# A decoder block on one core: the PLE projection is moved between the halves of the output projection, with three smaller reorderings

## The chip, the cores and the metric

The kernel is one program on one core of a Trainium2 chip. The metric is the device time of one execution in microseconds (us). Before the change it is 344.85 us, the median of three runs (344.47 to 345.8). The profile shown here is of one further execution of the same kernel.

The core's engines run their own instruction streams in order and wait for each other through semaphores: TensorE (PE in the profile; PEld is its loading of weights), VectorE (DVE), ScalarE (ACT), GpSimd (POOL) and SyncE (SP), which here only issues DMA transfers.

## The reference

One transformer layer over 256 positions of width 1024, in float32:

```python
hn  = rmsnorm(h, g_attn)
qkv = hn @ w_in                                  # 1024 -> 3072, split into two groups of 8 heads
ya  = rmsnorm(merge_heads(dilated_mixture(qa, ka, va, slopes_a)), g_out_a)
yb  = rmsnorm(merge_heads(moba_attention(qb, kb, vb, slopes_b)), g_out_b)
h   = h + concatenate([ya, yb]) @ w_out
h   = h + square(relu(rmsnorm(h, g_mlp) @ w_up)) @ w_down      # 1024 -> 4096 -> 1024
gate = sigmoid(rmsnorm(h, g_ple) @ w_ple_gate + b_ple_gate)
h   = h + gate * (p @ w_ple_proj)                # p is 256 x 256: the per-layer embedding (PLE)
out = rmsnorm(h, g_final)
```

With 256 positions both attention groups are plain causal attention over 256 keys with a bias per head: for group A the ALiBi distance less the logarithm of how many of the three dilated branches hold the key, for group B the distance alone. The sum of squares behind each RMSNorm can be taken apart from the product it scales, which the kernel does throughout.

## The kernel before

**Split operands.** Every float32 matrix that enters a matmul is split into a high part (`hi`, a copy rounded to fp32r on ACT, L79 or L81) and a low part (`lo`, the rest, a subtraction on DVE, L86 or L88). A product is three matmuls (`mm3`, L209 to L211): hi by hi, hi by lo, lo by hi. Weights come in slabs of 1 MB through four raw buffers; a slab's load (L61, issued by SP) waits until the slab four places earlier has been split.

**Units.** The program is a list of units in the order in which PE works: the first (v of group A and q, k of pairs 0 and 1), q and k of pairs 2 and 3, v of group B, q and k of pairs 4 to 7 in two units, the output projection's half over group A (`o_steps(0)`), its half over group B (`o_steps(1)`), eight pairs of MLP units (up, down) with the PLE projection (`ple_steps`, 24 matmuls) after the first up unit, and two gate units. While a unit runs, the next unit's slabs are split.

**Attention.** A pair is two heads. For each of the eight pairs n: DVE scales q and k out of PSUM (L362), ACT and DVE split them (L366, L370), PE makes the scores (L400), DVE adds the bias and takes the minimum (L408, L411), ACT exponentiates (L418), DVE takes the reciprocal of the sums (L422), ACT and POOL scale the probabilities `pb` (L431, L429), PE transposes them (L451), ACT and DVE copy them out (L455), PE multiplies by v (L467, L468), ACT and DVE split the result y (L476, L485), and its squares are summed into `ysum` by POOL (L482). POOL also makes the bias tile of the next pair (L388, for group A also L390), in two buffers. At the end of each group `y_stats` sums `ysum` over partitions with PE (L330) and takes the power -0.5 on POOL (L241).

**What sets the order.** In the first six units the order on PE, DVE, ACT and POOL is written out: a planner keeps a clock that advances by a unit's cost per step, and each attention step is an event with a due time on that clock (`at`, `within`), issued in the program when the clock passes it. An engine then runs its instructions in that order, however late its inputs are. SP is not under this planner. After the sixth unit a scheduler orders the engines by itself.

**Start.** The first unit takes eight blocks k of x and weights as they arrive. `x_squares` sums the squares of x block by block (ACT L323, two buffers; DVE L324), and `x_stats` sums them over partitions on PE (L330) after step 30, that is between blocks 4 and 5.

**End.** `gate_out` (L793 to L820) closes each piece of the output: z, sigmoid, times `ple`, plus h, sum of squares, times the gain (POOL L809), and on a token tile's last piece the mean of squares (L813), its power -0.5 (POOL L814), the scaling (DVE L816, ACT L818, POOL L819) and two stores (L817, L820). Token tile 1 is last, in a piece of 256 columns.

Of the kernel before, what the change touches and what calls it, by code (L numbers as in the profile page):

```python
# [17 lines left out]
P = 128  # L18
S = 256
# [13 lines left out]
def block_kernel(ctx: ExitStack, tc: tile.TileContext, a: dict):  # L33
# [106 lines left out]
    def run_units(units):  # L140
        with tc.manual_schedule(engines=ORDERED):
            first_loads()
            first_splits()
            for i, u in enumerate(units[:6]):
                for s in units[i + 2].slabs:
                    s.load()
                for f in u.inserts.get(0, []):
                    f()
                if i:
                    t, d = clock[0], u.n * u.cost  # L150
                    pieces = [(s, p) for s in units[i + 1].slabs for p in range(s.n)]
                    for n, (s, p) in enumerate(pieces):
                        hi, lo = s.halves(p)
                        dt = d * (n / len(pieces) if i > 1 else 0.35 + 0.65 * n / len(pieces))
                        at(t + dt, hi)
                        at(t + dt + 1.1, lo)
                for j, step in enumerate(u.steps()):
                    if i:
                        clock[0] += u.cost
                        run_events(1e9)  # L160
                    for f in u.inserts.get(j + 1, []):
                        f()
            while any(e[2] for e in events):
                clock[0] = min(e[0] for e in events if e[2])
                run_events(1e9)
        for i, u in list(enumerate(units))[6:]:
# [25 lines left out]
    def first_splits():  # L192
        for k in range(KT):
            if k in (0, 1, 2, 4):
                x_split(k, k + (1 if k < 2 else 2))
            sv, sq = (slabs_in[u][k // 4] for u in range(2))
            for part in (slice(0, 0.5), slice(0.5, 1)) if k == 0 else [slice(0, 1)]:
                for f in sv.halves(k % 4, part):
                    f()
            for f in sq.halves(k % 4):  # L200
                f()
            if k == 4:
                x_split(6, 8)
            if k:
                x_squares({1: range(2), 2: range(2, 4), 4: range(4, 6), 5: range(6, 8)}.get(k, ()))
# [151 lines left out]
    def evac_qk(g, j, ps):  # L357
# [21 lines left out]
        at(max(t + dt + 2.4, 3.4 + 8.1 * n), lambda: scores(g, j), 0.75)  # L379
# [12 lines left out]
    def scores(g, j):  # L392
# [47 lines left out]
        if n < 7:  # L440
            within(5.2, lambda: make_bias((n + 1) // NPAIR, (n + 1) % NPAIR))
        within(7.4 if n < 7 else 6.2, lambda: turn(g, j), 0.7)
# [17 lines left out]
    def values(g, j):  # L460
# [29 lines left out]
        if j == NPAIR - 1:  # L490
            within(3.4, lambda: y_stats(g), 0.3)
# [85 lines left out]
    def late_pieces():  # L577
        for n in (2, 3):
# [6 lines left out]
             {30: [x_stats], 34: [x_diag] + early(0), 38: [x_bcast, lambda: make_bias(0, 0)], 41: early(1),  # L585
# [9 lines left out]
    hsum = st(4)  # L595

# [44 lines left out]
    class Lazy:  # L641
# [6 lines left out]
        Unit(slabs_out[:2], o_steps(0), None, 16, 0.681),  # L648
        Unit(slabs_out[2:], o_steps(1), {0: [alloc_aT2]}, 16),
# [6 lines left out]
    slab_ple = Slab(a["w_ple"], 2)  # L656
# [4 lines left out]
    def open_mlp():  # L661
# [6 lines left out]
        pT = m.tile([P, 2, S], F32, name="pTin")
        nc.sync.dma_start(pT, a["pT"])
        mp["p2"] = [m.tile([P, 2, S], F32R, name=f"p2{i}") for i in range(2)]  # L670
        nc.scalar.activation(mp["p2"][0], pT, AF.Copy)
        nc.vector.tensor_tensor(mp["p2"][1], pT, mp["p2"][0].bitcast(F32), op=ALU.subtract)
# [80 lines left out]
    def ple_steps():  # L753
        for t in range(2):
            for n in range(2):
                ps = bank()
                tok, col = slice(t * P, (t + 1) * P), slice(n * 512, (n + 1) * 512)
                for k in range(2):
                    mm3(ps, (mp["p2"][0][:, k, tok], mp["p2"][1][:, k, tok]),
                        (slab_ple.hi[:, k, col], slab_ple.lo[:, k, col]), k == 0, k == 1)  # L760
                    yield
                nc.scalar.copy(mp["ple"][:, t, col], ps)
# [23 lines left out]
    def gate_out(ps, t, i):  # L786
# [15 lines left out]
        nc.vector.tensor_tensor(sg, sg, mp["ple"][:, t, col], op=ALU.mult)  # L802
        nc.vector.tensor_tensor(h, h, sg, op=ALU.add)
        if last and t == 1:
            nc.vector.tensor_tensor_reduce(z, h, h, 1.0, 0.0, op0=ALU.mult, op1=ALU.add,
                                           accum_out=so[:, i : i + 1])
        else:
            nc.scalar.activation(z, h, AF.Square, accum_out=so[:, i : i + 1])
        nc.gpsimd.tensor_tensor(hg[:, col], h, gain[:, col], op=ALU.mult)  # L809
        if not last:  # L810
            nc.gpsimd.tensor_scalar(mean, so[:, i : i + 1], 1.0 / DM, mean if i else EPS, op0=ALU.mult, op1=ALU.add)
            return
        nc.vector.scalar_tensor_tensor(mean, so[:, i : i + 1], 1.0 / DM, mean, op0=ALU.mult, op1=ALU.add)  # L813
        nc.gpsimd.tensor_tensor(r, mean, mhalf[:, :1], op=ALU.pow)  # L814
        out = a["out"]
# [81 lines left out]
```

## Time and profile before

| what | value |
|---|---|
| median of three runs | 344.85 us |
| the profiled execution | 344.78 us, of which 343.0 us is the span from first to last instruction |
| busy PE, DVE, ACT, POOL | 329.6, 231.3, 205.0, 44.3 us |
| granted TensorE clock | mean 0.992 of full speed |
| chain that ended last | PE 76%, ACT 7%, DVE 6%, DMA 4%, POOL 3% |

A slice of the span in which PE shows 9 has no room to become shorter unless PE has less to do, and PE shows 9 nearly throughout. What an order can change is the time in which PE stands still: the waits, which the profile lists by line and by who ended them, and the tail after the last matmul. "Releaser" is the engine whose instruction ended a wait.

### The profile page before, as it was taken

Reading aid. Unit: us, or ns where it says so; the run is one execution under the profiler, and the core shown is the slowest. Engines: PE = TensorE matmul, PEld = TensorE weight load, DVE = VectorE, ACT = ScalarE, POOL = GpSimd, SP = SyncE. Lnnn points to the kernel's source line nnn. Section 1 sums busy time; section 2 is a strip of 40 time slices with the busy share of each in tenths; the row PEclk is TensorE's granted clock in tenths of the full one; section 3 lists DMA queues with packets and bytes.
Section 4 is the critical chain, followed back from the end, with each engine's and each line's share of the span. In section 5 each row is a group of like instructions: output and inputs, shape, how many; then the busy total and the mean of one; then the engine's idle time right before and its main releaser. Section 6 shows DMA issues by size and latency. Waiting matters only on the chain.

```text
span 343.0 us, 5168 instructions
## 1 busy us (share of the span) xinstructions
PE 329.6 (96%) x1932; PEld 282.3 (82%) x1932; DVE 231.3 (67%) x429; ACT 205.0 (60%) x402; POOL 44.3 (13%) x69
## 2 busy tenths in 40 slices
PE   8989999999998999999999999999999999999990
PEld 7879976899886788888888888888888888888890
DVE  3887966486666869768567585585755955658563
ACT  5775777757666767838354474463743836458431
POOL 0013147342122200000000000000000000000443
PEclk9999999999999999999999999999999999999996
DMA  7998864242436449553727528356193472700011
GB/s 201 367 350 332 302 224 138 107 137 112 149 106 204 144 166 333 185 218 125 259 109 257 232 53 316 124 196 263 38 345 139 139 248 105 246 0 1 2 61 61
DMA packets 10969, 60.84 MB, mean 177 GB/s; under 512 B 1216, under 2 KB 1984, under 8 KB 4416
## 3 DMA queue, kind: packets, MB, share of 16 engines
q1 hardware_dynamic: 10944, 60.51, 49.9%
q8 instruction: 15, 0.25, 0.3%
q14 instruction: 10, 0.08, 0.1%
HBM read 59.46 MB, written 1.05 MB: 176 GB/s over the span
## 4 chain that ended last, share of the span: by engine, by line
PE 76%; ACT 7%; DVE 6%; DMA 4%; POOL 3%; issue 2%; SPq 1%; POOLq 0%; DVEq 0%; ACTq 0%
PE ps L697 17%; PE ps L209 15%; PE ps L211 15%; PE ps L210 15%; PE ps L698 9%; DMA raw<-in_w_in 4%; DVE lo L86 2%; ACT pb L418 2%; ACT hi L79 2%; POOL pb L429 1%; PE ps L400 1%; PE ps L451 1%; PE ps L618 1%; DVE qklo L370 1%; POOL bias L390 1%
## 5 line engine op out<-in xcount | busy, mean ns | idle before, releaser
L86 DVE TENSOR_TENSOR lo<-raw,hi 128x1024 fp32r<-128x1024 f32 (+2 forms) x75 | 81.0, 1101 | 37.3 <-ACT hi L79 37.2
L697 PE MATMUL ps<-h,hi 128*128 128x512 f32 x256 | 90.9, 399 | 0.0
L79 ACT ACTIVATE hi<-raw 128x1024 fp32r<-128x1024 f32 (+2 forms) x75 | 69.3, 949 | 33.6 <-PE ps L211 27.2
L698 PE MATMUL ps<-h,lo 128*128 128x256 f32 x256 | 71.9, 281 | 0.0
L88 DVE SCALAR_TENSOR_TENSOR lo<-raw,head,hi 128x512 fp32r<-128x512 f32 x80 | 56.8, 748 | 10.1 <-ACT hi L81 10.1
L81 ACT ACTIVATE hi<-raw,head 128x512 fp32r<-128x512 f32 x80 | 53.0, 714 | 12.7 <-PE ps L211 6.9
L697 PEld LDWEIGHTS ps<-h,hi 128*128 128x128 f32 x256 | 48.1, 188 | 11.8
L209 PE MATMUL ps<-hi,u 128*128 128x512 f32 x128 | 50.3, 393 | 0.0
L211 PE MATMUL ps<-hi,u 128*128 128x512 f32 x128 | 50.0, 390 | 0.0
L210 PE MATMUL ps<-lo,u 128*128 128x512 f32 x128 | 49.9, 390 | 0.0
L698 PEld LDWEIGHTS ps<-h,lo 128*128 128x128 f32 x256 | 48.4, 189 | 0.3
L209 PE MATMUL ps<-x,hi 128*128 128x256 f32 x128 | 37.4, 292 | 0.4 <-ACT hi L79 0.4
L211 PE MATMUL ps<-x,lo 128*128 128x256 f32 x128 | 36.2, 283 | 0.2 <-DVE lo L86 0.2
L210 PE MATMUL ps<-x,hi 128*128 128x256 f32 x128 | 36.1, 282 | 0.0
L241 POOL TENSOR_TENSOR stat<-stat,mhalf 128x2 f32<-128x2 f32 x5 | 4.4, 875 | 227.4 <-DVE stat L240 227.4
L211 PEld LDWEIGHTS ps<-hi,u 128*128 128x128 f32 x128 | 24.0, 188 | 5.2
L209 PEld LDWEIGHTS ps<-hi,u 128*128 128x128 f32 x128 | 24.0, 188 | 5.0
L210 PEld LDWEIGHTS ps<-lo,u 128*128 128x128 f32 x128 | 24.1, 188 | 4.7
L209 PEld LDWEIGHTS ps<-x,hi 128*128 128x128 f32 x128 | 24.4, 191 | 1.8 <-ACT hi L79 0.7
L211 PEld LDWEIGHTS ps<-x,lo 128*128 128x128 f32 x128 | 24.4, 191 | 0.4 <-DVE lo L86 0.4
L210 PEld LDWEIGHTS ps<-x,hi 128*128 128x128 f32 x128 | 24.4, 191 | 0.2
L678 ACT COPY r<-ps 128x256 f32<-128x256 f32 x32 | 11.8, 367 | 19.7 <-PE ps L698 19.6
(130 smaller groups left out, 514.0 us busy)
## 6 DMA issues: line engine op xcount, KB each, us to landing
raw<-in_w_up SPq DMA_DIRECT2D x16, 1024.0 KB, 5.1
raw<-in_w_down SPq DMA_DIRECT2D x16, 1024.0 KB, 4.8
raw<-in_w_in SPq DMA_DIRECT2D x8, 1024.0 KB, 5.5
raw<-in_w_out SPq DMA_DIRECT2D x4, 1024.0 KB, 4.7
raw<-in_w_gate SPq DMA_DIRECT2D x4, 1024.0 KB, 5.3
raw<-in_w_in SPq DMA_DIRECT2D x4, 512.0 KB, 9.2
raw<-in_w_in SPq DMA_DIRECT2D x7, 256.0 KB, 6.5
h_sb<-in_x SPq DMA_DIRECT2D x1, 1024.0 KB, 6.9
```

What stands on the lines that cost most here:

```text
L79: nc.scalar.activation(h, r, AF.Copy)
L81: nc.scalar.activation(h, r, AF.Copy, scale=sc)
L86: nc.vector.tensor_tensor(l, r, h.bitcast(F32), op=ALU.subtract)
L88: nc.vector.scalar_tensor_tensor(l, r, sc, h.bitcast(F32), op0=ALU.mult, op1=ALU.subtract)
L209: nc.tensor.matmul(ps, lhs[0], rhs[0], start=start, stop=False)
L210: nc.tensor.matmul(ps, lhs[0], rhs[1], start=False, stop=False)
L211: last_mm[0] = nc.tensor.matmul(ps, lhs[1], rhs[0], start=False, stop=stop)
L241: nc.gpsimd.tensor_tensor(r, ms, mhalf[:, :n], op=ALU.pow)
L418: nc.scalar.activation(pb[:, h, sl], sc[:, h, sl], AF.Exp, bias=nm[:, 0, c], scale=-1.0, accum_out=nm[:, 1, c])
L678: nc.scalar.copy(b, ps[:, S:])
L697: nc.tensor.matmul(ps, s.hi[:, k % 4, col], aT2[2][:, k], start=k == 0, stop=False)
L698: last_mm[0] = nc.tensor.matmul(ps[:, S:], s.lo[:, k % 4, col], aT2[0][:, k], start=False, stop=k == KT - 1)
```

## The change

The PLE projection becomes a unit between the two halves of the output projection, and joins the planned units (seven instead of six). Its weights are loaded and its input p is loaded and split earlier, through buffers of the attention (`qk`, `qkhi`, `qklo`). The sum over partitions of group B's squares moves from right behind the last pair to step 2 of `o_steps(1)`. The bias of the next pair is made 0.8 after a pair's scores on the planner's clock instead of 5.2, which is ahead of the scaling of the probabilities. Scores are due 0.8 later than before, and the last pair's transposes 1.2 later. The squares of x blocks 4 to 7 are added together with block 4, and `x_stats` goes from step 30 to step 33. In the last piece the mean is folded into the reduction, the multiplication by the gain goes from POOL to DVE, the scaling is split 640 to 384 columns between DVE and ACT, and a token tile is stored once.

```diff
-            for i, u in enumerate(units[:6]):
+            for i, u in enumerate(units[:7]):
...
-                x_squares({1: range(2), 2: range(2, 4), 4: range(4, 6), 5: range(6, 8)}.get(k, ()))
+                x_squares({1: range(2), 2: range(2, 4), 4: range(4, 8)}.get(k, ()))
...
-        at(max(t + dt + 2.4, 3.4 + 8.1 * n), lambda: scores(g, j), 0.75)
+        at(max(t + dt + 3.2, 3.4 + 8.4 * n), lambda: scores(g, j), 0.75)
...
-            within(5.2, lambda: make_bias((n + 1) // NPAIR, (n + 1) % NPAIR))
-        within(7.4 if n < 7 else 6.2, lambda: turn(g, j), 0.7)
+            within(0.8, lambda: make_bias((n + 1) // NPAIR, (n + 1) % NPAIR))
+        within(7.4, lambda: turn(g, j), 0.7)
...
-        if j == NPAIR - 1:
-            within(3.4, lambda: y_stats(g), 0.3)
+        if j == NPAIR - 1 and g == 0:
+            within(3.6, lambda: y_stats(g), 0.3)
...
-             {30: [x_stats], 34: [x_diag] + early(0), 38: [x_bcast, lambda: make_bias(0, 0)], 41: early(1),
+             {33: [x_stats], 37: [x_diag] + early(0), 41: [x_bcast, lambda: make_bias(0, 0)], 43: early(1),
...
+    slab_ple = Slab(a["w_ple"], 2)
+    ple = outer.tile([P, 2, DM], F32, name="ple")
+    p2 = []
+
+    def p_load():
+        p2.append(ap.tile([P, 2, S], F32, tag="qk", name="pT", bufs=2))
+        nc.sync.dma_start(p2[0], a["pT"])
...
+            nc.scalar.activation(p2[1], p2[0], AF.Copy)
...
+            nc.vector.tensor_tensor(p2[2], p2[0], p2[1].bitcast(F32), op=ALU.subtract)
+        within(7.0, hi)
+        within(8.0, lo)
...
-        Unit(slabs_out[:2], o_steps(0), None, 16, 0.681),
-        Unit(slabs_out[2:], o_steps(1), {0: [alloc_aT2]}, 16),
+        Unit(slabs_out[:2], o_steps(0), {2: [p_load]}, 16, 0.681),
+        Unit([slab_ple], lambda: ple_steps(), None, 8, 0.681),
+        Unit(slabs_out[2:], o_steps(1), {0: [alloc_aT2], 2: [lambda: y_stats(1)]}, 16),
...
-        nc.vector.tensor_scalar(hg[:, :512], hg[:, :512], r, None, op0=ALU.mult)
-        nc.sync.dma_start(out[t, :, :512], hg[:, :512])
-        nc.scalar.activation(hg[:, 768:], hg[:, 768:], AF.Copy, scale=r)
-        nc.gpsimd.tensor_scalar(hg[:, 512:768], hg[:, 512:768], r, 1.0, op0=ALU.mult, op1=ALU.mult)
-        nc.sync.dma_start(out[t, :, 512:], hg[:, 512:])
+
+        nc.vector.tensor_tensor_reduce(z, h, h, 1.0 / DM, mean, op0=ALU.mult, op1=ALU.add,
+                                       accum_out=so[:, i : i + 1])
+        nc.gpsimd.tensor_tensor(r, so[:, i : i + 1], mhalf[:, :1], op=ALU.pow)
+        nc.vector.tensor_tensor(hg[:, col], h, gain[:, col], op=ALU.mult)
+        nc.vector.tensor_scalar(hg[:, :640], hg[:, :640], r, None, op0=ALU.mult)
+        nc.scalar.activation(hg[:, 640:], hg[:, 640:], AF.Copy, scale=r)
+        nc.sync.dma_start(a["out"][t], hg)
...
-    units.append(Unit([slab_ple], ple_steps, None, 8))
```

Three places where the instructions stand in another order. The first is GpSimd from the first unit's statistics to pair 1's probabilities, before (a row is line, operation, output and inputs by the program's names; `bias` and `pb` carry a buffer number, one per pair):

```order
L241 TENSOR_TENSOR stat_102<-stat_102,mhalf_103 128x2
L388 TENSOR_SCALAR bias_376<-consts_132 128x256
L390 TENSOR_TENSOR bias_376<-bias_376,consts_132 128x256
...
L429 TENSOR_SCALAR pb_481<-pb_481,nm_482 128x128 x2
L388 TENSOR_SCALAR bias_555<-consts_132 128x256
L390 TENSOR_TENSOR bias_555<-bias_555,consts_132 128x256
...
L429 TENSOR_SCALAR pb_604<-pb_604,nm_605 128x128 x2
```

and now:

```order
L241 TENSOR_TENSOR stat_102<-stat_102,mhalf_103 128x2
L388 TENSOR_SCALAR bias_386<-consts_132 128x256
L390 TENSOR_TENSOR bias_386<-bias_386,consts_132 128x256
...
L388 TENSOR_SCALAR bias_494<-consts_132 128x256
L390 TENSOR_TENSOR bias_494<-bias_494,consts_132 128x256
...
L429 TENSOR_SCALAR pb_482<-pb_482,nm_483 128x128 x2
L388 TENSOR_SCALAR bias_616<-consts_132 128x256
L390 TENSOR_TENSOR bias_616<-bias_616,consts_132 128x256
...
L429 TENSOR_SCALAR pb_607<-pb_607,nm_608 128x128 x2
```

Pair 1's bias stood behind pair 0's probabilities; it now stands ahead of them, right behind pair 0's bias.

The second is PE from pair 7's products with v to the output projection's second half, before (`y0hi` and `y0lo` are group A's y, `y_1113` group B's):

```order
L468 MATMUL ps_1382<-pT,vt 64x128
L209 MATMUL ps_1375<-hi,y0hi 128x512
L210 MATMUL ps_1375<-lo,y0hi 128x512
L211 MATMUL ps_1375<-hi,y0lo 128x512
...
L330 MATMUL ps_1399<-ones,ysum_141 128x1 x2
L209 MATMUL ps_1408<-hi,y_1113 128x512
```

and now (`p2hi` and `p2lo` are the split input of the PLE projection, `y_1111` group B's y):

```order
L468 MATMUL ps_1399<-pT,vt 64x128
L209 MATMUL ps_1392<-hi,p2hi 128x512
L210 MATMUL ps_1392<-lo,p2hi 128x512
...
L211 MATMUL ps_1437<-hi,p2lo 128x512
L209 MATMUL ps_1452<-hi,y_1111 128x512
...
L330 MATMUL ps_1465<-ones,ysum_141 128x1 x2
L209 MATMUL ps_1452<-hi,y_1111 128x512
```

The product L330 with `ysum` had 6 matmuls between it and pair 7's last product with v; it now has 27, 21 of the PLE projection and 6 of the second half. Further ahead, pair 7's transposes had 21 wide matmuls (128x512) between them and the pair's scores, and now have 27. Ahead of pair 6's scores, from the end of its q and k, 27 narrow matmuls (128x256) of pair 7 stand instead of 18.

The third is DVE at the very end, before:

```order
L802 TENSOR_TENSOR sg<-sg,ple 128x256
L803 TENSOR_TENSOR h_sb<-h_sb,sg 128x256
L805 ISA z,stat<-h_sb 128x256
L805 ISA stat 128x1
L813 SCALAR_TENSOR_TENSOR stat<-stat 128x1
L816 TENSOR_SCALAR hg<-hg,stat 128x512
```

and now:

```order
L813 TENSOR_TENSOR sg<-sg,ple 128x256
L814 TENSOR_TENSOR h_sb<-h_sb,sg 128x256
L821 ISA z,stat<-h_sb,stat 128x256
L821 ISA stat 128x1
L824 TENSOR_TENSOR hg<-h_sb,bg 128x256
L825 TENSOR_SCALAR hg<-hg,stat 128x640
```

The mean's own instruction is gone, a multiplication stands in its place, and the scaling is a quarter wider.

## Rows read from the trace of the kernel before

**Rows 1.** Waits of PE: engine, line, releaser: us in total, times, longest.

```profile
PE ps L451 <- POOL pb L429: 1.8, 2, 1.1
PE ps L330 <- DVE xsq L324: 1.0, 1, 1.0
PE ps L330 <- POOL ysum L482: 0.5, 1, 0.5
PE ps L400 <- DVE qklo L370: 0.3, 1, 0.3
```

**Rows 2.** Timeline, PE, first statistics: start, us, what, [idle before, releaser].

```profile
22.04 0.60 PE L330 MATMUL ps<-ones,xsq 128*128 128x1 f32 x4 [1.04 <-DVE xsq L324]
22.51 0.48 PE L209 MATMUL ps<-hi,x 128*128 128x512 f32 x1
```

**Rows 3.** Timeline, ACT and DVE, squares of blocks 4 and 5.

```profile
18.24 0.71 ACT L323 ACTIVATE sq<-xT 128x256 f32<-128x256 f32 x2
...
18.97 0.95 DVE L324 TENSOR_TENSOR xsq<-xsq,sq 128x256 f32<-128x256 f32 x2
19.83 0.69 DVE L86 TENSOR_TENSOR lo<-raw,hi 128x512 fp32r<-128x512 f32 x1
```

**Rows 4.** Timeline, POOL and PE, pair 0's probabilities and transposes.

```profile
41.73 1.65 POOL L429 TENSOR_SCALAR pb<-pb,nm 128x128 f32<-128x128 f32 x2 [12.77 <-DVE nm L422]
...
43.09 0.90 PE L451 MATMUL ps<-ident,pb 128*128 128x128 f32 x6
```

**Rows 5.** Timeline, DVE and POOL, pair 1.

```profile
46.99 0.43 DVE L408 CUSTOM_DVE_ANT_0 sc<-ps,bias 128x256 f32<-128x256 f32 x1 [0.67 <-POOL bias L390]
...
51.19 1.68 POOL L429 TENSOR_SCALAR pb<-pb,nm 128x128 f32<-128x128 f32 x2 [4.23 <-DVE nm L422]
```

**Rows 6.** Line 429: count, shortest, median, longest in ns.

```profile
L429 POOL TENSOR_SCALAR pb<-pb,nm x16: 367/372/1443, 41.7 to 108.0; 128x128 f32<-128x128 f32 x16
```

**Rows 7.** Timeline, PE, pair 6's scores.

```profile
90.46 0.39 PE L400 MATMUL ps<-qkhi 64*128 64x256 f32 x2
91.19 0.39 PE L400 MATMUL ps<-qklo,qkhi 64*128 64x256 f32 x2 [0.34 <-DVE qklo L370]
91.41 0.28 PE L400 MATMUL ps<-qkhi,qklo 64*128 64x256 f32 x2
```

**Rows 8.** Timeline, PE, wide matmuls and pair 7's transposes.

```profile
106.39 0.39 PE L210 MATMUL ps<-lo,y0hi 128*128 128x512 f32 x1
106.62 0.39 PE L211 MATMUL ps<-hi,y0lo 128*128 128x512 f32 x1
108.11 0.90 PE L451 MATMUL ps<-ident,pb 128*128 128x128 f32 x6 [1.10 <-POOL pb L429]
```

**Rows 9.** Timeline, DVE, POOL and SP, after the last matmul.

```profile
336.99 0.42 DVE L805 CUSTOM_DVE_ANT_0 z<-h_sb 128x256 f32<-128x256 f32 x1
...
337.54 0.48 DVE L813 SCALAR_TENSOR_TENSOR stat<-stat 128x1 f32<-128x1 f32 x1
...
338.09 0.55 POOL L814 TENSOR_TENSOR stat<-stat,mhalf 128x1 f32<-128x1 f32 x1
338.68 0.49 DVE L816 TENSOR_SCALAR hg<-hg,stat 128x512 f32<-128x512 f32 x1 [0.67 <-POOL stat L814]
...
339.62 0.38 SPq L820 DMA_DIRECT2D out<-hg  x1
```

**Rows 10.** DMA issues: count, KB each, median us from issue to landing.

```profile
out<-hg SPq DMA_DIRECT2D x4, 256.0 KB, 2.1
...
pTin<-in_pT SPq DMA_DIRECT2D x1, 256.0 KB, 5.0
```

**Rows 11.** Timeline, SP and ACT: loads of the first up weights, pair 6's squares.

```profile
85.54 7.14 SPq L61 DMA_DIRECT2D raw<-in_w_up  x2
...
105.08 0.37 ACT L481 ACTIVATE sq<-ps 128x256 f32<-128x256 f32 x1
```

**Rows 12.** Window from group B's output projection to the first down unit: busy us.

```profile
114.50:146.00 31.50, 31.50 (x165) 26.71 (x165) 24.83 (x44) 22.56 (x43) 1.82 (x2) 1.00 0.64 219
```

More of the change, by code (lines that the diff above doesn't have):

```diff
@@ L165, in run_units @@
                 run_events(1e9)
-        for i, u in list(enumerate(units))[6:]:
+        for i, u in list(enumerate(units))[7:]:
             for s in units[i + 2].slabs if i + 2 < len(units) else []:
@@ L595, in block_kernel, with hi, lo @@
     hsum = st(4)
+    slab_ple = Slab(a["w_ple"], 2)
[4 more added lines that the diff above has]
+        nc.sync.dma_start(p2[0], a["pT"])
+        def hi():
+            p2.append(ap.tile([P, 2, S], F32R, tag="qkhi", name="p2hi", bufs=3))
+            nc.scalar.activation(p2[1], p2[0], AF.Copy)
+        def lo():
+            p2.append(ap.tile([P, 2, S], F32R, tag="qklo", name="p2lo", bufs=3))
+            nc.vector.tensor_tensor(p2[2], p2[0], p2[1].bitcast(F32), op=ALU.subtract)
+        within(7.0, hi)
+        within(8.0, lo)
     def o_steps(g):
@@ L655, in block_kernel @@
     slabs_dn = [[Slab(a["w_down"][2 * u + i], 2) for i in range(2)] for u in range(NU)]
-    slab_ple = Slab(a["w_ple"], 2)
     slabs_gt = [[Slab(a["w_gate"][n, :, 4 * i : 4 * i + 4], 4, g=3, k0=4 * i) for i in range(2)] for n in range(2)]
@@ L664, in open_mlp @@
         m = mp["p"]
-        mp["ple"] = m.tile([P, 2, DM], F32, name="ple")
         mp["bg"] = m.tile([P, 2, DM], F32, name="bg")
         nc.sync.dma_start(mp["bg"], bass.AP(tensor=a["bg"].tensor, offset=a["bg"].offset, ap=[[0, P], [DM, 2], [1, DM]]))
[L668 to L672, printed above, removed]
     def act(u, q, ps):
@@ L758, in ple_steps @@
                 for k in range(2):
-                    mm3(ps, (mp["p2"][0][:, k, tok], mp["p2"][1][:, k, tok]),
+                    mm3(ps, (p2[1][:, k, tok], p2[2][:, k, tok]),
                         (slab_ple.hi[:, k, col], slab_ple.lo[:, k, col]), k == 0, k == 1)
                     yield
-                nc.scalar.copy(mp["ple"][:, t, col], ps)
+                nc.scalar.copy(ple[:, t, col], ps)
     fin = {}
@@ L801, in gate_out @@
         h = h_sb[:, t, col]
-        nc.vector.tensor_tensor(sg, sg, mp["ple"][:, t, col], op=ALU.mult)
+        nc.vector.tensor_tensor(sg, sg, ple[:, t, col], op=ALU.mult)
         nc.vector.tensor_tensor(h, h, sg, op=ALU.add)
[L804 to L807, printed above, removed]
+        if not last:
             nc.scalar.activation(z, h, AF.Square, accum_out=so[:, i : i + 1])
-        nc.gpsimd.tensor_tensor(hg[:, col], h, gain[:, col], op=ALU.mult)
-        if not last:
+            nc.gpsimd.tensor_tensor(hg[:, col], h, gain[:, col], op=ALU.mult)
             nc.gpsimd.tensor_scalar(mean, so[:, i : i + 1], 1.0 / DM, mean if i else EPS, op0=ALU.mult, op1=ALU.add)
             return
-        nc.vector.scalar_tensor_tensor(mean, so[:, i : i + 1], 1.0 / DM, mean, op0=ALU.mult, op1=ALU.add)
-        nc.gpsimd.tensor_tensor(r, mean, mhalf[:, :1], op=ALU.pow)
-        out = a["out"]
-        nc.vector.tensor_scalar(hg[:, :512], hg[:, :512], r, None, op0=ALU.mult)
-        nc.sync.dma_start(out[t, :, :512], hg[:, :512])
-        nc.scalar.activation(hg[:, 768:], hg[:, 768:], AF.Copy, scale=r)
-        nc.gpsimd.tensor_scalar(hg[:, 512:768], hg[:, 512:768], r, 1.0, op0=ALU.mult, op1=ALU.mult)
-        nc.sync.dma_start(out[t, :, 512:], hg[:, 512:])
+        nc.vector.tensor_tensor_reduce(z, h, h, 1.0 / DM, mean, op0=ALU.mult, op1=ALU.add,
[5 more added lines that the diff above has]
+        nc.sync.dma_start(a["out"][t], hg)
     units.append(Unit(slabs_up[0], up_steps(0), {8: [r2_stats]}, 32))
-    units.append(Unit([slab_ple], ple_steps, None, 8))
     for u in range(1, NU):
```

## The prediction

> **What bounds the kernel.** I read the busy times and slices of the page first: PE is at work nearly throughout, and the matmuls stay the same in number and form, so time can come only from where PE stands still. That is the view of PE's waits, read next [rows 1]. Leaving out the very start it names four causes: the transposes wait for POOL's scaling of the probabilities (1.8 us in two waits, the longer 1.1), the sum of x's squares waits for DVE (1.0), the sum of group B's squares waits for POOL (0.5), one pair's scores wait for DVE's low part (0.3). Together 3.6 us, about 1% of the run. After that I read the timeline at each of these places, and at the end of the span, where no matmul is left and a single file of small operations runs into the last store [rows 9].
>
> A wait costs PE a little more than its own length. At pair 6's scores the starts 90.46 and 91.19 are 0.73 apart where 0.22 is usual there (91.19 to 91.41), and the wait is 0.34: 0.17 goes with the restart [rows 7]. At pair 7's transposes it is 1.49 from 106.62 to 108.11, less 0.23 between two wide matmuls and less the wait of 1.10: 0.16 [rows 8]. I add 0.17 to each wait that goes.
>
> **The change part by part.**
>
> *Squares with block 4, statistics at step 33: 0.* PE reached the statistics at 22.04 - 1.04 = 21.00 and waited; block 5 began at 22.51 [rows 2]. Now block 5's v product comes first. Its second matmul needs the low part of that piece, which DVE began at 19.83 behind two adds (0.95) and takes up behind four: 18.97 + 2 x 0.95 = 20.87, and 0.69 for the piece gives 21.6 [rows 3]. The squares on ACT keep up: with two buffers the last one starts once the second add is over, at 19.92, and takes about 0.36. So PE trades a wait of 1.04 for one of about 0.6, and the product with the squares (0.47, from 22.04 to 22.51) comes later without a wait. PE gains 0.5 to 1.0 here. I do not count it, because of what is late next: pair 0's transposes started at 43.09 and took 0.90 for six, since the second half waited for POOL, which scaled from 41.73 to 43.38 [rows 4]. That scaling follows the split, reduction and exponentials on DVE and ACT, whose first operations start behind weight pieces and the broadcast of the statistics, and the latter does not come earlier. PE arrives sooner and waits longer. If the chain does move with PE, up to 1.0 more is saved.
>
> *Bias ahead of the probabilities: 0.87.* Pair 1's second reduction waited 0.67 on DVE for its bias, until 46.99 [rows 5], since POOL made it after pair 0's probabilities. Now POOL makes it in the idle time before them (12.77 us idle at that point [rows 4]). Pair 1's reduction ends some 0.8 earlier, and with it the scaling at 51.19 that its transposes waited for. That wait is the 1.8 - 1.1 = 0.7 of [rows 1]; with the restart 0.87. The price: bias and DVE's splits now run side by side more. Two scalings of pair 0 took 1.65 and of pair 1 1.68, though the median of one is 0.372 and the longest 1.443 [rows 4 to 6], so an operation on POOL can stand 1.07 longer, and a bias of four operations could be some us late. It has a whole pair's period to spare, so I set this at 0.
>
> *Scores 0.8 later on the planner's clock: 0.51.* Nine more narrow matmuls lie between pair 6's q and k and its scores than before. At half of the wide ones' 0.23 each [rows 8] that is 1.0 us, over the wait of 0.34 + 0.17 [rows 7].
>
> *Pair 7's transposes later: 1.27.* Six more wide matmuls stand between its scores and its transposes: 6 x 0.23 = 1.38 against 1.10 + 0.17 [rows 8]. It covers by only 0.1, so half of the term may stay.
>
> *PLE in between: 0.67.* Group B's sum of squares now has 21 more matmuls ahead of it, 21 x 0.23 = 4.8 us against a wait of 0.5 + 0.17 [rows 1, 8]. The PLE projection's own 24 matmuls (5.5 us) only move. What rides on it: p's load stands behind the first up slab in SP's queue. The up slabs were issued from 85.54 to 92.68 [rows 11]; the one in front now waits for the same release as the second then, so p is issued at about 92.7 and lands 5.0 later [rows 10], near 98. ACT takes p's high part behind pair 6's squares, at 105.45 [rows 11], and ahead of pair 7's probabilities; 7 us of cover, and beyond it each us of lateness is one of PE. The second half's weights are now split during PLE: four pieces on DVE in 5.5 us, and the last is needed 2 us into the next unit.
>
> *The end: 0.1.* Without the mean's own instruction the power can start at 336.99 + 0.42 and the 0.07 that lay between the mean and the power, 337.48 in place of 338.09, 0.61 sooner [rows 9]. The scaling of 640 columns takes up to 0.49 x 640 / 512 = 0.61 in place of 0.49. The single store is issued when that ends: 337.48 + 0.55 + 0.04 + 0.61 = 338.7. Before, the last issue was at 339.62 and landed 2.1 later, at 341.7 [rows 9, 10]. For 512 KB no row shows the landing: from 2.1 (256 KB at the end) to 5.0 (256 KB in a full queue) [rows 10]. I take 2.7, near the first, since the two stores of before were themselves 0.4 apart. That gives 341.4, a gain of 0.3. If the power waits out the new multiplication (about 0.42, as the reduction of the same size [rows 9]; a scaling waited 1.07 in [rows 6]) it is a loss of 0.1. I take 0.1; the ends are a gain of 0.9 (landing 2.1, no waiting) and a loss of 3.1 (POOL 1.07 late, landing 5.0).
>
> On this overlap the Trainium skill has a rule that speaks against the change ("SBUF — State Buffer", section "Who interferes with whom"): a DVE instruction with two inputs in SBUF and a GpSimd instruction that reads SBUF share a read interface, and the one that comes second waits until the first is through. The trace agrees, in that scalings of 0.372 stood up to 1.443 [rows 6]. By the rule the power at the end waits for the whole multiplication, the last term is -0.1, and the sum below is 0.2 less.
>
> **The sum.** 0 + 0.87 + 0.51 + 1.27 + 0.67 + 0.1 = 3.4 us off the profiled execution's 344.78 (span 343.0 and 1.8 around it) is 341.4. The median of the runs is 0.07 above that execution, which I leave out. Forecast: 341.4 us.
>
> **The rivals.**
>
> *The waits come back inside the attention.* DVE and ACT run the pairs in a fixed order; if their chain and not PE's order sets the pace, as at pair 0, PE meets it again one pair on. For it: the low part of pair 6 and pair 1's reduction were late on DVE itself. Against it: the waits for the bias on DVE's path do go. Then only the last pair, the group's sum and the end remain, 1.27 + 0.67 + 0.1 = 2.0: 342.7 us.
>
> *The order does not do what it says.* The planner's clock is not the engines': pair 7's scaling comes as much later as its transposes, since p's low part and two evacuations now stand near it on DVE. New waits equal the old: 344.8 us.
>
> *Slower: DVE becomes the bound from the output projection's second half to the second up unit.* Before, this stretch and PLE had 31.5 us and DVE worked 24.83 of them, 79% [rows 12]. PLE's 5.5 us leave the stretch and its splitting work mostly stays, so it must fit into 26.0. It does if DVE fills 95%. If DVE reaches only the 79% it showed, the stretch takes 31.5 us again: 5.5 lost against 3.4 won, 346.9 us. It decides from 5.1 us of new waiting of PE there (a DVE share of 80%). Against it: PLE's own pieces and p leave the stretch with it, and the up slabs' splits of later units look far ahead.
>
> **How the numbers follow.** What a measurement of this kernel can tell from no change is about 0.5%, 1.7 us: below 343.1 is faster, above 346.6 slower. The forecast has 0.66 (its own range 339.9 to 342.5), the waits that come back 0.20 (three quarters of it faster), no effect 0.07, the slower rival 0.07. So faster 0.66 + 0.15 = 0.81, same 0.05 + 0.07 = 0.12, slower 0.07. The range goes from 339.7, where the start's 1.0 and part of the end's 0.9 come on top, to 344.0, past the first rival and part of the end's loss.
>
> **What would show it.** In the profile after: no wait of PE for `ysum`, pair 1's and pair 7's transposes without a POOL wait over 0.3; a wait of PE near 21 us for a low part in place of the squares; pair 0's transposes at about 43 as before, although PE is early; DVE's reductions without POOL as their releaser; the power beginning about 337.5 - 3.3 = 334.2 and one store per tile. Wrong would be: a PE wait over 0.5 for a low part or for p between 95 and 140 us, a PE that arrives early at pair 0 and does not wait, or a last store that lands more than 3.5 us after its issue.

## The result and the profile after

The changed kernel takes 341.12 us (median of four runs, 340.58 to 341.58), the kernel before 345.18 us (median of four runs, 344.47 to 345.8; the fourth of them raised the median from 344.85): a ratio of 0.9874, 95% interval 0.9858 to 0.9891. That is 4.1 us faster. The forecast was 341.4 us, 3.4 us less than the profiled execution before. The profiled execution took 341.23 us, with a span of 339.4 where it was 343.0, at a granted clock of 0.994 (0.992 before).

PE's waits after the change, the whole list (engine, line, releaser: us in total, times, longest), which answers to [rows 1]:

```profile
PE ps L451 <- POOL pb L429: 1.1, 1, 1.1
PE ps L220 <- DVE mhalf L229: 1.0, 1, 1.0
PE ps L209 <- ACT hi L79: 0.9, 1, 0.9
PE ps L210 <- DVE lo L86: 0.5, 2, 0.2
PE ps L211 <- DVE lo L86: 0.2, 1, 0.2
```

The waits for `xsq`, `ysum` and `qklo` are gone. L220 stands ahead of the first unit, in both kernels; L209, L210 and L211 wait in the first 23 us for the high and low parts of weights. One wait in the steady part is left, and it stands at pair 0, where no wait was seen before [rows 4]. The timeline of POOL, DVE and PE around it, as parts in order of time (start, us, what, [idle before, releaser]):

```profile
32.53 1.58 POOL L390 TENSOR_TENSOR bias<-bias,consts 128x256 f32<-128x256 f32 x1
...
33.44 1.22 DVE L370 TENSOR_TENSOR qklo<-qk,qkhi 128x512 fp32r<-128x512 f32 x1
...
42.49 1.23 DVE L86 TENSOR_TENSOR lo<-raw,hi 128x1024 fp32r<-128x1024 f32 x1
...
42.65 1.66 POOL L429 TENSOR_SCALAR pb<-pb,nm 128x128 f32<-128x128 f32 x2 [8.54 <-DVE nm L422]
...
44.01 0.91 PE L451 MATMUL ps<-ident,pb 128*128 128x128 f32 x6 [1.11 <-POOL pb L429]
```

Pair 0's transposes start at 44.01, 0.92 later than at 43.09. The bias of pair 1, now made early, is the first row: while POOL subtracts, DVE's low part next to it takes 1.22 us. In the kernel before nothing ran on POOL there, and the same instruction took 0.68:

```profile
33.06 0.68 DVE L370 TENSOR_TENSOR qklo<-qk,qkhi 128x512 fp32r<-128x512 f32 x1
```

That is 0.54 of the 0.92. The other 0.38 is not the change: weights were late in this run (the wait of 0.9 on L209 at 12.16), and the first 128x512 product of block 3 stands at 15.59 where it stood at 15.21, 0.38 later, ahead of anything that the change moves. Such starts differ from run to run: in the experiments below PE's waits on L209 add up to anything from 0 to 1.4 us.

At pair 1 the loss is made good. DVE's reductions follow each other without POOL, which answers to [rows 5], and PE's transposes run without a wait:

```profile
46.35 0.41 DVE L408 CUSTOM_DVE_ANT_0 sc<-ps,bias 128x256 f32<-128x256 f32 x1
...
46.90 0.42 DVE L408 CUSTOM_DVE_ANT_0 sc<-ps,bias 128x256 f32<-128x256 f32 x1
...
52.67 0.82 PE L451 MATMUL ps<-ident,pb 128*128 128x128 f32 x6
```

Equal work can be followed by its start, before and after: pair 0's transposes 43.09 and 44.01 (0.92 lost), pair 1's products with v 55.82 and 55.84 (even again), the first matmul of the output projection 96.59 and 95.50 (1.09 won), the first down unit 155.38 and 152.21 (3.17 won), the last matmul 334.79 and 331.57 (3.22), the end of the span 343.0 and 339.4 (3.6). The output projection and the first down unit on PE, before:

```profile
96.59 0.40 PE L209 MATMUL ps<-hi,y0hi 128*128 128x512 f32 x1
...
155.38 0.40 PE L209 MATMUL ps<-hi,u 128*128 128x512 f32 x1
```

and now:

```profile
95.50 0.40 PE L209 MATMUL ps<-hi,y0hi 128*128 128x512 f32 x1
...
152.21 0.40 PE L209 MATMUL ps<-hi,u 128*128 128x512 f32 x1
```

From 44.01 on no row of PE's timeline up to the first down unit shows a wait. From PLE's first matmul to 142 us, 1.1 us into the second up unit, PE is busy throughout (window, us: length, PE, PEld, DVE, ACT, POOL busy, clock, DMA share, GB/s). This answers to [rows 12], whose window ends in the second up unit too (it began at 144.09 before) and not at the first down unit:

```profile
109.86:142.00 32.14, 32.14 (x172) 26.77 (x171) 27.75 (x44) 25.12 (x47) 3.00 (x3) 1.00 0.71 249
```

The tail, which answers to [rows 9, 10], on DVE, POOL, ACT and SP, and the landing of the stores:

```profile
333.88 0.48 DVE L821 CUSTOM_DVE_ANT_0 z<-h_sb,stat 128x256 f32<-128x256 f32 x1
...
334.29 0.42 DVE L824 TENSOR_TENSOR hg<-h_sb,bg 128x256 f32<-128x256 f32 x1
...
334.46 0.67 POOL L823 TENSOR_TENSOR stat<-stat,mhalf 128x1 f32<-128x1 f32 x1 [1.56 <-DVE stat L821]
...
335.16 0.62 ACT L826 ACTIVATE hg<-hg,stat 128x384 f32<-128x384 f32 x1 [2.34 <-POOL stat L823]
...
335.80 0.34 SPq L827 DMA_DIRECT2D out<-hg  x1
...
out<-hg SPq DMA_DIRECT2D x2, 512.0 KB, 2.6
```

From the start of the last matmul to the end of the span it is 7.83 us (339.4 - 331.57) where it was 8.21. The last store was issued 4.23 us behind that start, where it was 4.83.

### The profile page after: what moved, and what is told of

Same layout as the page of the kernel before. It is cut to its first block, busy times and chain, and to the rows that moved or that the text cites. A ratio compares the mean times of both kernels' runs of the same rounds, so it can differ in the third digit from the quotient of the medians.

```text
span 339.4 us, 5168 instructions
## 1 busy us (share of the span) xinstructions
PE 328.1 (97%) x1932; PEld 281.8 (83%) x1932; DVE 233.1 (69%) x431; ACT 204.9 (60%) x400; POOL 43.1 (13%) x65
## 4 chain that ended last, share of the span: by engine, by line
PE 84%; DVE 5%; DMA 4%; ACT 2%; issue 1%; SPq 1%; POOL 1%; POOLq 0%; DVEq 0%; ACTq 0%
PE ps L708 18%; PE ps L209 17%; PE ps L210 17%; PE ps L211 17%; PE ps L709 9%; DMA raw<-in_w_in 3%; PE ps L400 2%; DVE lo L86 2%; PE ps L451 2%; PE ps L467 1%; DMA xT<-in_xT 1%; PE ps L635 1%; DVE qklo L370 1%; ACT hi L79 1%; PE ps L468 1%
## 5 line engine op out<-in xcount | busy, mean ns | idle before, releaser
L209 PE MATMUL ps<-hi,u 128*128 128x512 f32 x128 | 50.3, 393 | 0.0
L211 PE MATMUL ps<-hi,u 128*128 128x512 f32 x128 | 49.9, 390 | 0.0
L210 PE MATMUL ps<-lo,u 128*128 128x512 f32 x128 | 49.9, 390 | 0.0
L209 PE MATMUL ps<-x,hi 128*128 128x256 f32 x128 | 37.5, 293 | 0.0
L211 PE MATMUL ps<-x,lo 128*128 128x256 f32 x128 | 36.3, 283 | 0.2 <-DVE lo L86 0.2
L210 PE MATMUL ps<-x,hi 128*128 128x256 f32 x128 | 36.2, 283 | 0.0
L211 PEld LDWEIGHTS ps<-hi,u 128*128 128x128 f32 x128 | 24.0, 188 | 5.2
L209 PEld LDWEIGHTS ps<-hi,u 128*128 128x128 f32 x128 | 24.0, 188 | 5.0
L210 PEld LDWEIGHTS ps<-lo,u 128*128 128x128 f32 x128 | 24.1, 188 | 4.7
L209 PEld LDWEIGHTS ps<-x,hi 128*128 128x128 f32 x128 | 24.4, 191 | 1.5 <-issue 0.5
L211 PEld LDWEIGHTS ps<-x,lo 128*128 128x128 f32 x128 | 24.4, 191 | 0.4 <-DVE lo L86 0.4
L210 PEld LDWEIGHTS ps<-x,hi 128*128 128x128 f32 x128 | 24.4, 191 | 0.3
```

The source lines that it names most:

```text
L209: nc.tensor.matmul(ps, lhs[0], rhs[0], start=start, stop=False)
L210: nc.tensor.matmul(ps, lhs[0], rhs[1], start=False, stop=False)
L211: last_mm[0] = nc.tensor.matmul(ps, lhs[1], rhs[0], start=False, stop=stop)
```

## Experiments: one part of the change at a time

Each of these is the kernel before with one part. In all experiments the kernel before ran on the same chip (medians 345.2 to 345.4); the ratios are to it.

**start_only.** The squares with block 4 and the statistics at step 33.

```diff
-x_squares({1: range(2), 2: range(2, 4), 4: range(4, 6), 5: range(6, 8)}.get(k, ()))
+x_squares({1: range(2), 2: range(2, 4), 4: range(4, 8)}.get(k, ()))
-{30: [x_stats], 34: [x_diag] + early(0), 38: [x_bcast, ...], 41: early(1),
+{33: [x_stats], 37: [x_diag] + early(0), 41: [x_bcast, ...], 43: early(1),
```

> The kernel before with one part of the change: the squares of blocks 4 to 7 added with block 4, and the statistics of x and what follows them three steps later. Theory: the chain on DVE and ACT sets when pair 0's probabilities are ready, so PE's wait of 1.0 us for the squares goes, a wait of 0.4 to 0.7 for a low part comes near 21 us, and PE then waits at pair 0's transposes, which start at 43.1 as before, or up to 0.4 later since the broadcast of the statistics comes later; the time is that of before within 0.4 us. Rival: PE's own order sets the start, pair 0's transposes come 0.5 to 1.0 us earlier, and so does the end.

344.73 us, ratio 0.9996 (0.9983 to 1.0008): nothing. The wait of 1.0 for `xsq` is not in its list, and PE's waits for POOL at the transposes are 2.2 us in three where they were 1.8 in two: what PE wins at the statistics it waits out at pair 0, where the new wait is 0.52 us.

**bias_only.** Only the due time of the bias.

```diff
-within(5.2, lambda: make_bias((n + 1) // NPAIR, (n + 1) % NPAIR))
+within(0.8, lambda: make_bias((n + 1) // NPAIR, (n + 1) % NPAIR))
```

> The kernel before with one part of the change: the next pair's bias made 0.8 after a pair's scores on the planner's clock. Theory: GpSimd's four bias operations for pair 1 now run beside DVE's splits of q and k and stretch one of them from 0.68 to about 1.2 us, so pair 0's transposes come 0.5 us later; pair 1's wait for GpSimd (0.7) goes; net 0.3 to 0.5 us faster. Rival, as forecast: no cost at pair 0, 0.87 us faster.

344.57 us, ratio 0.9979 (0.9967 to 0.9991): 0.7 us faster (0.3 to 1.1). Pair 1's wait is gone, and a new one stands at pair 0; the list has two waits of the transposes, 1.5 us in all (0.37 at pair 0, 1.1 at pair 7). In this run the bias fell beside another operation than in the changed kernel: on DVE a split of weights took 1.60 us in place of 1.23, pair 0's low part kept its 0.68, and pair 0's transposes came 0.40 later, counted from the first 128x512 product of block 3.

**scores_only.** Only the due time of the scores.

```diff
-at(max(t + dt + 2.4, 3.4 + 8.1 * n), lambda: scores(g, j), 0.75)
+at(max(t + dt + 3.2, 3.4 + 8.4 * n), lambda: scores(g, j), 0.75)
```

> The kernel before with the scores' due times alone (3.2 and 8.4 n). As forecast: the wait of the score products on the query's and key's low part (L400 on VectorE) goes, 0.5 us, 344.7 us against 345.2. Theory B, from the other single parts: it is worth 0.7, since the start of the first output unit came 1.1 us earlier in the changed kernel and the bias gives 0.4 of it by then: 344.5 us. Rival: the scores placed later only push the probabilities and the transposes, 345.2 us or more.

343.44 us, ratio 0.995 (0.9932 to 0.9969): 1.7 us faster (1.1 to 2.3), beyond every expectation. Three things show in its trace. First, the low part held up the scores of three pairs before, not of one: two pauses were too short for the list of waits. The scores of pairs 4 and 5 in the kernel before, on PE:

```profile
73.64 0.39 PE L400 MATMUL ps<-qkhi 64*128 64x256 f32 x2
74.02 0.39 PE L400 MATMUL ps<-qklo,qkhi 64*128 64x256 f32 x2
...
81.48 0.38 PE L400 MATMUL ps<-qkhi 64*128 64x256 f32 x2
81.78 0.39 PE L400 MATMUL ps<-qklo,qkhi 64*128 64x256 f32 x2
```

The starts are 0.38 and 0.30 apart where 0.22 is usual, and the restart costs again, about 0.1 each: from its first matmul to the next other work a pair's scores took 1.10, 1.01 and 1.45 us, and take 0.83, 0.83 and 0.84 in the changed kernel. That is 1.06 us in place of the 0.51 that was forecast from the one wait in the list. Second, the wait of pair 7's transposes is gone though their due time is as before, and though a split still stands beside POOL's scaling (1.52 us): DVE took the reciprocal at 105.28, 6.03 us behind pair 6's transposes, where it was 7.19 (106.53 less 99.34). Third, part of that comes back at the next wait, the one for `ysum`:

```profile
PE ps L330 <- POOL ysum L482: 1.1, 1, 1.1
```

It was 0.5 [rows 1].

**turn_only.** Only the due time of pair 7's transposes.

```diff
-within(7.4 if n < 7 else 6.2, lambda: turn(g, j), 0.7)
+within(7.4, lambda: turn(g, j), 0.7)
```

> The kernel before with pair 7's transposes due at 7.4 alone; no PLE unit follows, so pair 7's values products stay ahead of the second output unit. Theory A (three different parts of the change each remove the same wait): the 1.1 us wait goes, time 344.1 to 344.3 us against 345.3. Theory B (without the PLE unit the time is lost again, at the values products and at the row sums of the second half): 344.9 to 345.3 us.

346.39 us, ratio 1.0035 (1.0015 to 1.0054): 1.2 us slower (0.5 to 1.9), outside both theories. The twelve executions differ with their granted clock: at a mean of 0.994 three took 345.1 to 345.4 us, as the kernel before, and at 0.985 three took 348.2 to 348.4. The profiled one (0.990) took 346.59 us. The six matmuls moved ahead of the transposes do take their wait away, but they were the six that stood between pair 7's products with v and the sum over `ysum`. On PE:

```profile
108.50 0.82 PE L451 MATMUL ps<-ident,pb 128*128 128x128 f32 x6
...
111.32 0.66 PE L467 MATMUL ps<-pT,vt 128*64 128x256 f32 x4
111.80 0.40 PE L468 MATMUL ps<-pT,vt 128*64 128x128 f32 x4
114.18 0.61 PE L330 MATMUL ps<-ones,ysum 128*128 128x1 f32 x4 [1.99 <-POOL ysum L482]
...
115.66 0.39 PE L210 MATMUL ps<-lo,y 128*128 128x512 f32 x1
115.89 0.45 PE L211 MATMUL ps<-hi,y 128*128 128x512 f32 x1
116.14 0.63 PE L209 MATMUL ps<-hi,y 128*128 128x512 f32 x1
116.56 0.63 PE L210 MATMUL ps<-lo,y 128*128 128x512 f32 x1
```

The wait for `ysum` is 1.99 us in place of 0.5 [rows 1], which eats the gain of 1.27. And two microseconds behind it PE itself slows: the same matmul takes 0.63 us, and starts are 0.42 apart in place of 0.23. In a table by windows of this run the clock column (0.51) shows why:

```profile
114.18:116.00 1.82, 1.82 (x10) 1.60 (x11) 1.18 (x3) 1.51 (x3) 0.94 (x1) 1.00 0.00 0
116.00:119.50 3.50, 3.50 (x10) 2.73 (x9) 2.13 (x4) 0.00 (x0) 0.20 (x1) 0.51 0.80 255
119.50:123.00 3.50, 3.50 (x19) 2.84 (x18) 1.67 (x3) 1.24 (x4) 0.00 (x0) 1.00 0.58 159
```

The granted clock stood at the lower of its two levels, 1.2 GHz, for about 3.4 us, in which eight matmuls were begun: 8 x (0.425 - 0.23) = 1.6 us lost beside the wait.

**ple_only.** The PLE unit between the halves, `y_stats(1)` at step 2 of the second half; due times and tail as before, but for group A's `y_stats`, due at 3.6 as in the changed kernel.

```diff
-Unit(slabs_out[:2], o_steps(0), None, 16, 0.681),
-Unit(slabs_out[2:], o_steps(1), {0: [alloc_aT2]}, 16),
+Unit(slabs_out[:2], o_steps(0), {2: [p_load]}, 16, 0.681),
+Unit([slab_ple], lambda: ple_steps(), None, 8, 0.681),
+Unit(slabs_out[2:], o_steps(1), {0: [alloc_aT2], 2: [lambda: y_stats(1)]}, 16),
...
```

> The kernel before with one part of the change: the PLE projection between the halves of the output projection, with the sum of group B's squares behind it; pair 7's transposes stay due at 6.2. Theory: the wait for that sum (0.5) goes, the wait at pair 7's transposes (1.1) stays, 0.67 us faster, and no new wait of PE over 0.3 between 110 and 150 us. Rival: with the PLE projection's 5.5 us gone from behind the first up unit DVE becomes the bound there, PE waits for low parts between 115 and 150 us, and the time is that of before or up to 2 us longer.

343.02 us, ratio 0.9941 (0.992 to 0.9961): 2.0 us faster (1.3 to 2.8), three times the term. The wait for `ysum` is gone as forecast, and that of pair 7's transposes too, with their old due time. Why shows on DVE and POOL behind pair 7's reciprocal. The kernel before:

```profile
106.62 1.20 DVE L86 TENSOR_TENSOR lo<-raw,hi 128x1024 fp32r<-128x1024 f32 x1
...
106.88 1.52 POOL L429 TENSOR_SCALAR pb<-pb,nm 128x128 f32<-128x128 f32 x2 [0.55 <-DVE nm L422]
```

and this one, with PE's transposes:

```profile
107.68 0.72 POOL L429 TENSOR_SCALAR pb<-pb,nm 128x128 f32<-128x128 f32 x2 [0.56 <-DVE nm L422]
...
108.10 0.90 PE L451 MATMUL ps<-ident,pb 128*128 128x128 f32 x6
```

While the first half runs, the next unit's weights are split, and that unit is now PLE with one slab in place of the second half with two. So no split stands on DVE beside POOL's scaling, and two scalings take 0.72 us in place of 1.52. Seen from pair 6's transposes, POOL also starts 0.4 us earlier (7.14 behind them, 7.54 before): 0.8 and 0.4 make up the wait; this is read off the two traces, and no run separates the two. 1.27 + 0.67 = 1.94 is the gain that was forecast for two parts; one part gives it.

**tail_only.** The last piece alone.

```diff
-nc.vector.tensor_tensor_reduce(z, h, h, 1.0, 0.0, ...)
...
+nc.sync.dma_start(a["out"][t], hg)
```

> The kernel before with one part of the change: the end (mean folded into the reduction, gain on DVE, scaling on DVE and ACT, one store). Theory: the power starts 0.5 to 0.6 us sooner after the last matmul and is lengthened by 0.1 by the multiplication beside it, the one store of 512 KB lands in 2.6; 0.4 us faster. Rival: the power waits out the whole multiplication (0.42), the time is that of before or 0.1 longer.

344.78 us, ratio 0.9993 (0.9979 to 1.0008): not to be told from nothing by its time. In the trace the tail from the last matmul's start is 7.89 us against 8.21, 0.3 shorter.

## Experiments: one part undone in the changed kernel

**after_turn_early** (the due time 6.2 for pair 7 again):

> The changed kernel with pair 7's transposes due at 6.2 again (all else kept). Theory A (the wait of pair 7's transposes is gone with the PLE unit and with the later scores already, as each of these alone removed it; the due time adds nothing): no wait at those transposes, 341.1 us as the changed kernel, within 0.3. Theory B, the forecast (the later due time is what removes the 1.1 us wait): the wait returns, 342.2 to 342.4 us.

340.73 us, ratio 0.9864 (0.9848 to 0.9879), with no wait at pair 7's transposes. Theory A held: the later due time adds nothing. That the time is 0.4 lower comes from the start, as far as the profile shows: pair 0's transposes stand at 42.94, 1.07 earlier than in the changed kernel's, and from them to the end of the span it is 295.4 us in both.

**after_scores_early** (2.4 and 8.1 n again):

> The changed kernel with the scores' due times of before (2.4 and 8.1 n; all else kept). Theory A (of the 1.8 us that the later scores gave alone, 1.2 was the wait of pair 7's transposes, which the PLE unit removes too; the rest is theirs): 341.7 us. Forecast: the wait for the low part, 0.5 us, returns: 341.6 us. Theory B (the later scores are worth as much as alone): 342.9 us.

342.16 us, ratio 0.9902 (0.9885 to 0.9919), 1.0 us slower than the changed kernel. That lies between the theories at 341.7 and 342.9. In its trace the scores of pairs 4, 5 and 6 take 0.89, 0.99 and 1.44 us, together 0.82 more than in the changed kernel (1.06 more in the kernel before).

**bias1_late** (pair 1's bias behind pair 0's probabilities again):

```diff
-within(0.8, lambda: make_bias(...))
+within(5.2 if n == 0 else 0.8, lambda: make_bias(...))
```

> The changed kernel, with pair 1's bias alone put back behind pair 0's probabilities on GpSimd (all other parts kept). Theory A (GpSimd's subtraction, the 1.58 us of L390, stretches VectorE's L370 from 0.68 to 1.22 us and so makes pair 0's transposes 0.54 late): L370 is back to about 0.68 us, the transposes of pair 0 wait about 0.6 in place of 1.1 us, but the wait before pair 1's transposes (0.7 us) returns, so the time is 341.1 to 341.5 us, no gain. Theory B (the bias costs VectorE nothing, and the 1.1 us wait came from later data alone): pair 0's wait stays 1.1 us, pair 1's wait returns, 341.9 us.

341.14 us, ratio 0.9882 (0.9868 to 0.9897): as the changed kernel. Theory A held in each of its parts (DVE, then PE):

```profile
33.22 0.68 DVE L370 TENSOR_TENSOR qklo<-qk,qkhi 128x512 fp32r<-128x512 f32 x1
...
43.24 0.90 PE L451 MATMUL ps<-ident,pb 128*128 128x128 f32 x6 [0.50 <-POOL pb L429]
...
53.07 0.55 PE L451 MATMUL ps<-ident,pb 128*128 128x128 f32 x3 [0.68 <-POOL pb L429]
```

DVE is back to 0.68 us, pair 0's wait falls from 1.11 to 0.50, and pair 1's 0.68 is back. Pair 1's products with v stand 0.30 later than in the changed kernel, counted in the same way; the medians, 0.02 apart, do not resolve that.

**after_two_stores** (a token tile stored in 640 and 384 columns):

```diff
-nc.sync.dma_start(a["out"][t], hg)
+nc.sync.dma_start(a["out"][t, :, :640], hg[:, :640])
+nc.sync.dma_start(a["out"][t, :, 640:], hg[:, 640:])
```

> The changed kernel with two stores per tile at the end (640 and 384 columns) in place of one, the addition shared by VectorE and ACT as in the changed kernel. Theory A (the end of the one store, 2.6 us, against the 2.1 us of a smaller one, pays for one more issue of 0.3 us): 341.0 to 341.2 us, no difference. Theory B (the last store's size sets the end): the last store takes 2.2 us, time 340.7 us.

341.41 us, ratio 0.988 (0.9866 to 0.9895): no difference by the time. In the trace the tail from the last matmul's start is 8.0 us against 7.8. The smaller stores land in 2.3 and 2.2 us, the whole one in 2.6, and the second issue stands 0.38 behind the first.

## Experiments: the wait that was left

**scale0_vector** (pair 0's scalings on DVE):

```diff
-nc.gpsimd.tensor_scalar(pb[:, h, sl], pb[:, h, sl], r, 1.0, ...)
+(nc.vector if n == 0 else nc.gpsimd).tensor_scalar(pb[:, h, sl], pb[:, h, sl], r, 1.0, ...)
```

> The changed kernel, with pair 0's two 128x128 scalings (L429) on VectorE in place of GpSimd, in the program right behind the reciprocal and so ahead of the weights' split. Theory A (GpSimd's scaling is held from 42.65 until VectorE's split of 42.49 to 43.72 ends, 1.66 us where two alone take 0.74): the transposes of pair 0 start 0.4 to 0.7 us earlier, their wait is 0.4 to 0.7 in place of 1.1 us, time 340.4 to 340.8 us. Theory B (the scalar engine's share or the chain ahead of the reciprocal sets the end): the wait stays about 1.1 us, its releaser becomes ACT, time 341.1 us.

341.11 us, ratio 0.9876 (0.9859 to 0.9894): no gain, and more than the place of the scalings changed. With the two scalings gone from POOL's queue, pair 2's bias, which stood behind them, moved ahead and ran beside DVE's split and low part ahead of the reciprocal:

```profile
39.92 1.65 DVE L86 TENSOR_TENSOR lo<-raw,hi 128x1024 fp32r<-128x1024 f32 x1
41.49 0.88 DVE L370 TENSOR_TENSOR qklo<-qk,qkhi 128x512 fp32r<-128x512 f32 x1
...
42.50 0.74 DVE L429 TENSOR_SCALAR pb<-pb,nm 128x128 f32<-128x128 f32 x2
```

The two took 1.22 and 0.69 in the changed kernel. The wait fell to 0.8 only, now for DVE, and pair 1's transposes wait 0.34 for POOL.

**turn0_later** (pair 0's transposes due at 8.5, so that pair 1's scores stand ahead of them):

```diff
-within(7.4, lambda: turn(g, j), 0.7)
+within(8.5 if n == 0 else 7.4, lambda: turn(g, j), 0.7)
```

> The changed kernel, with pair 0's transposes due at 8.5 in place of 7.4, so that pair 1's score products (0.84 us of TensorE) stand ahead of them. Theory A (TensorE only lacked other work there, the 1.1 us are free to fill): the wait falls to 0.2 to 0.4 us, time 340.2 to 340.5 us. Theory B (the chain through pair 1's probabilities sets the end of this stage, whatever stands ahead of pair 0's transposes): the wait moves to pair 1's transposes, 341.0 to 341.3 us.

339.8 us (339.14 to 340.09), ratio 0.984 (0.9825 to 0.9855): 1.3 us faster than the changed kernel, more than theory A gave it, and the fastest of all. PE and POOL:

```profile
43.66 0.39 PE L400 MATMUL ps<-qkhi 64*128 64x256 f32 x2
...
44.50 0.88 PE L451 MATMUL ps<-ident,pb 128*128 128x128 f32 x6
...
50.19 0.72 POOL L429 TENSOR_SCALAR pb<-pb,nm 128x128 f32<-128x128 f32 x2 [2.19 <-DVE nm L422]
...
51.42 0.81 PE L451 MATMUL ps<-ident,pb 128*128 128x128 f32 x6
```

The wait is filled with work that was ready, and no transposes wait any more. The gain is the 1.11 us of the wait and a little more: pair 1's chain starts earlier too, and its scalings meet no split (0.72 us, where they took 1.68 at 51.09 in the changed kernel).

## Why the prediction was right, and where it was not

The total was right: 341.4 forecast, 341.12 measured. The reading behind it was right too: only PE's pauses could give time, and nearly all of them were the ones in [rows 1]. But of the six terms two are right as they stand, three have another size, and one names the wrong cause. That the sum came so close is partly luck: the bias gave 0.5 less than its term, and the scores 0.55 more.

*Start, 0.* Right, and for the reason given: PE arrived earlier at pair 0 and waited there. That it waited there before already, as the prediction reads from the 0.90 us of the six transposes, is not borne out: the list of waits before has none at pair 0, and in turn0_later, with the scaling over, the six took 0.88. The new wait for the low part is 0.23 us in the list, not 0.6; by the starts, 21.32 and 22.05, the pause is 0.50 over the usual 0.23.

*Bias, 0.87.* The gain at pair 1 was 0.90 (0.92 late at pair 0's transposes, 0.02 at pair 1's products with v). The failed step is "so I set this at 0", the price beside DVE. It was looked for on POOL, where there was time to spare, and fell on DVE: 0.54 us on pair 0's low part, on the path to pair 0's transposes. What remains is 0.36 by the trace (0.3 to 1.1 by bias_only, where the price was 0.40).

*Scores, 0.51.* The mechanism was right and the size was not: 1.06 (by after_scores_early 1.0 in time and 0.82 in the trace). The term was made from the one wait in the list, but two more pairs had pauses of 0.16 and 0.08, each with the price of a restart, 0.1.

*Pair 7's transposes, 1.27.* The wait went, but not through the due time. turn_only lost 1.2 us, and after_turn_early lost nothing. The step that failed is to take the six matmuls as free: alone they do cover the wait, but they were already the cover of the next one, and in the changed kernel no wait was left for them. The wait came from POOL's scaling beside a split on DVE, and the PLE unit takes that split away; later scores remove the wait too, by an earlier reciprocal.

*PLE, 0.67.* The size of its own wait was right. It carries the 1.27 as well: 1.94 by the two terms, 2.08 by the trace (3.17 less 1.09), and 2.0 in ple_only. p was issued at 92.00 (92.7 forecast), and nothing waited for it.

*The end, 0.1.* 0.38 by the trace. Landing was 2.6, near the 2.7 taken. The store was issued 0.60 sooner after the last matmul, not 0.92: the power began 0.2 later than taken, and took 0.67 us beside DVE's multiplication, 0.12 more than [rows 9].

The rule that was weighed there, that of the Trainium skill ("SBUF — State Buffer", section "Who interferes with whom"), by which the second operation waits until the first is through, comes near the trace in three places. At the end the multiplication is over at 334.71, one power more makes 335.26, and the power was over at 335.13. At pair 0 the split ends at 43.72, one scaling more makes 44.09, and the transposes start at 44.01; POOL's subtraction ends at 34.11, one low part more makes 34.79, and the low part was over at 34.66. Each is about 0.1 us sooner than a full wait, and the measurement decides. The price at the end was small not because the two ran freely side by side, but because the power began 0.17 us into the multiplication and only 0.25 of it was left; the prediction had put a wait at the whole 0.42.

Term by term: 0.36 + 1.06 + 2.08 + 0.38 = 3.88, less 0.38 for the late weights of the profiled run is 3.5; the span became 3.6 shorter. The 0.1 between them is not assigned.

Of the rivals, the slower one failed on its condition: it needed DVE to fill at most 80% of the stretch, DVE filled 27.75 of 32.14 us, 86%, and PE did not wait. The one by which pair 7's scaling comes as much later as its transposes failed too: DVE took the reciprocal 6.04 us behind pair 6's transposes (104.97 less 98.93), where it was 7.19. The waits that come back inside the attention did come, once, at pair 0. That changes with an order are not additive is shown by the parts: alone they won 0.15 + 0.7 + 1.7 - 1.2 + 2.0 + 0.2, about 3.6 us against 4.1 together, and that is near only because pair 7's wait, counted twice (scores, PLE), and the loss of turn_only, which the PLE unit covers, cancel.

## What to carry to other kernels

Ask of a wait not only which work could stand in front of it, but which other wait that work covers now: six matmuls moved past pair 7's transposes opened a wait of 2 us behind them. Look for what stretched the releaser as well: here two scalings took 1.52 us in place of 0.72 because a split ran beside them, and taking that split away was worth more than covering the wait. A due time is best spent where ready work can fill the gap, as pair 1's scores did for pair 0's transposes.

## What the runs showed of the hardware

POOL and DVE slow each other in both directions: in the changed kernel a scaling of 0.37 us took up to 1.34 beside a split, a low part of 0.68 took 1.22 beside POOL's subtraction, and in scale0_vector a split of 1.22 took 1.65 beside POOL's bias.

In the profile of turn_only a pause of 1.99 us on PE was followed, about 2 us after PE had resumed, by some 3.4 us at a granted clock of 0.51; the pause of 1.11 us in the changed kernel was not, as its windows around 44.01 show:

```profile
40.00:44.00 4.00, 2.90 (x25) 2.70 (x23) 3.69 (x6) 3.61 (x10) 1.35 (x2) 1.00 1.06 372
44.00:48.00 4.00, 3.99 (x34) 3.24 (x36) 3.26 (x11) 3.13 (x7) 3.54 (x5) 1.00 0.76 248
```

With the slow stretch the longer pause cost nearly twice its length. It need not come each time: three of the twelve executions of turn_only had a mean clock of 0.994 and lost nothing; they were not profiled.

A store of 512 KB landed in 2.6 us and one of 192 KB in 2.2, but the second store had to be issued 0.38 behind the first, and the tail was 0.2 longer with two: splitting the store gained nothing.
